# One core, a hybrid decoder layer: head 0 by quarter products, a stacked operand for the sample's pooling columns, small rows on another queue

## The chip, the cores and the metric

The kernel runs on one core of one Trainium2 chip. The metric is the device time of one execution in microseconds (us), the median of several runs. TensorE (PE) multiplies, VectorE (DVE), ScalarE (ACT) and GpSimd (POOL) do the elementwise work, and DMAs are issued from the queues of SyncE (SP) and of ScalarE. All numbers are float32. A product of two float32 matrices is made of three products of a faster format: each operand is split into a rounded part `hi` and the remainder `lo`, and `hi*hi + hi*lo + lo*hi` are summed in PSUM.

## The reference, cut to what matters

```python
u = x * (1 + scale1) + shift1            # scale1, shift1 from silu(c) @ w_ada + b_ada
z = u @ w_in                             # columns: pool | q | f | i | out_gate | gate_A | gate_B
# A: pooling over the "pool" columns;  B: per head a recurrence from q, f, i, then norm and out_gate
f = lb + (1.0 - lb) * sigmoid(z_f);  q = silu(z_q);  v = z_i
merged = sigmoid(z_ga) * (y_pool @ w_a) + sigmoid(z_gb) * (y_hgrn @ w_b)
x = layer_norm(ALPHA * x + g1 * (merged @ w_out))
x = layer_norm(ALPHA * x + g2 * (silu(h @ w_gate) * (h @ w_up)) @ w_down)   # h = x*(1+scale2)+shift2
```

There is one prompt of 512 tokens and a sample group of 8 times 8 = 64 tokens, 576 columns in all; the model width is 1024, with 8 heads of 128.

## The kernel before

The weights pass once from HBM through SBUF; activations stand transposed, channels on the partitions and the 576 tokens (`T`) along the row. `UH` and `UL` (L247, L248) are the two parts of `u`, in eight row blocks `kt`.

**The start (L94 to L430).** SP's queue carries, in this order of the program: the conditioning rows `cc`, the first half of x, the first block of `w_ada`, six small loads into the tile `rows` (biases, norm weights; L282 to L285), the next block of `w_ada`, the first slice of `w_in`, and then further blocks of `w_ada`, x and `w_in`. PE transposes x and `rows`, multiplies `c` by `w_ada` in pairs of blocks (`ada1`, L359), and the results `mod` give scale and shift. For b = 0 to 3 the loop at L389 makes two row blocks of `u` with their parts, calls `ada1` for the next b, and multiplies the two blocks by the 512 pooling columns of `w_in` into five accumulators `ps0` (tile `zp`, L417): four of 128 prompt tokens and one of the 64 sample tokens, three products of 512 columns each. VectorE also makes the sums `ta`, `tb`, `tc_` of blocks of `u` (L420 to L425), which `split` (L171) parts into `TU["t1"]`, `"t2"`, `"t4"` and later `"t3"`.

**Head 0 (L484 to L516 and L755 to L766).** The four column blocks f, q, i, out_gate of head 0 are made by `gemm` (L158): eight row blocks times three products times two column halves (256 and 320), 48 matmuls each. The weight of a `gemm` comes by `load_w` (L114): one load and one split (ACT a cast, DVE a difference). Between the four stand the pooling products `mix(0)` to `mix(3)` (L463), and then the elementwise work `ev_f`, `ev_q`, `ev_qd` of head 0's recurrence. The load of f is held until the last block of `w_ada` is issued (`late`, L493).

**Heads 1 to 7 (from L767).** Two column blocks at a time are made by `fast_u` (L744) and `fast` (L220): with weights and activations cut in quarters, seven products of 12 matmuls with 288 columns make both. The weights of such a pair, `fast_w` (L182) and `fast_q`, take two loads (the second into `rawu`, which has one buffer), four sums or differences of quarters (`s1` to `s4`; for these pairs on GpSimd), casts on ACT, and differences on DVE and GpSimd. They come into three buffers each of `whi` and `wlo`, in turn, and `hq`, `lq` with one. The pair after is prepared while one is multiplied. Inside the pairs stand the steps of the head before (`hg1` to `hg4`).

The order of instructions on each engine is fixed before the run: a planner simulates the program and places every instruction when it deems it ready, in the program's order of priority. On the chip each engine takes its instructions in that order and waits where an operand isn't there. The rest of the kernel (the gates, `w_b`, `w_out`, the feed-forward layer) is not touched.

Of the kernel before, what the change touches and what calls it, by code (L numbers as in the profile page):

```python
# [73 lines left out]
def trunk(tc, consts, x_prompt, x_sample, state_pool, state_hgrn, c_prompt, c_sample,  # L74
# [16 lines left out]
    U, _U = pl.open("u", "left")  # L91
    s0, _s0 = pl.open("s0", "right")
    sx, _sx = pl.open("sx", "right")
    cc = t_(s0, [9, D], "cc")  # L94
    sp.dma_start(out=cc[0:1], in_=c_prompt)
    sp.dma_start(out=cc[1:9], in_=c_sample)
    cst = t_(cp, [P, C_END], "cst")
    act.dma_start(out=cst, in_=consts[:, 0:C_END])
    ident = cst[:, C_ID:C_ID + P]
    rows = t_(s0, [92, P], "rows")  # L100
    R_LB, R_NW, R_PS, R_BA, R_LG, R_LO, R_END = 0, 16, 24, 28, 76, 84, 92
    cst_eps = t_(cp, [P, 2], "eps")
    dve.memset(cst_eps[:, 0:1], RMS_EPS)
    dve.memset(cst_eps[:, 1:2], LN_EPS)
# [174 lines left out]

    xin = [x_load(0)]  # L280
    ada_ready[SC1 // 2] = ada_load(s0, SC1 // 2)
    for r, src in ((R_BA, b_ada[0]), (R_LB, lb_logits.rearrange("r c -> (r c)")), (R_NW, hgrn_norm_w[0]),  # L282
                   (R_PS, pool_scale[0]), (R_LG, ln1_g[0]), (R_LO, ln1_b[0])):
        v = src.rearrange("(h p) -> h p", p=P)
        sp.dma_start(out=rows[r:r + v.shape[0]], in_=v)  # L285
    ada_ready[SH1 // 2] = ada_load(s0, SH1 // 2)
    w0 = [load_w(seq.pop(0))]
    ada_pre(1)
# [87 lines left out]
    dve.tensor_tensor(out=oml, in0=le1, in1=oml, op=ALU.mult)  # L376
    dve.tensor_scalar(out=noml, in0=oml, scalar1=-1.0, scalar2=None, op0=ALU.mult)

    YA = t_(ym, [P, 4, T], "ya")
    YB = t_(ym, [P, NH, T], "yb")  # L380


    ta = YB[:, 0:2].rearrange("p a (k n) -> p (a k) n", n=HT)
# [2 lines left out]
    def t_tiles(p, names):  # L386
        return {n: tuple(t_(p, [P, 4, HT], n + x, F32R) for x in "hl") for n in names}

    for b in range(4):  # L389
        us_ = []  # L390
        for kt in (2 * b, 2 * b + 1):

            sc, sh = mod[:, SC1 + kt], mod[:, SH1 + kt]
            u = YB[:, 2 + kt] if b < 2 else t_(s0, [P, T], "u32", bufs=2)
            us_.append(u)
            us = u[:, TP:T].rearrange("p (b l) -> p b l", b=NB)
            act.activation(out=UH[:, kt, 0:TP], in_=XT[:, kt, 0:TP], func=AF.Identity, scale=sc[:, 0:1], bias=sh[:, 0:1])
            dve.tensor_tensor(out=us, in0=XT[:, kt, TP:T].rearrange("p (b l) -> p b l", b=NB),
                              in1=bcast(sc[:, 1:9], LS), op=ALU.mult)
            dve.tensor_tensor(out=us, in0=us, in1=bcast(sh[:, 1:9], LS), op=ALU.add)  # L400
            dve.tensor_copy(out=UH[:, kt, TP:T], in_=u[:, TP:T])
            act.activation(out=u[:, 0:TP], in_=XT[:, kt, 0:TP], func=AF.Identity, scale=sc[:, 0:1], bias=sh[:, 0:1])
            dve.tensor_tensor(out=UL[:, kt], in0=u, in1=UH[:, kt].bitcast(F32), op=ALU.subtract)
        if b < 3:
            ada1(b + 1)
        if b == 0:
            x_turn(1)
            pl.close(_sx)
            tu, _tu = pl.open("tu", "left")
            TU = t_tiles(tu, ("t1", "t2", "t4"))  # L410
        for kt in (2 * b, 2 * b + 1):
            hi, lo = (half(x, kt % 2) for x in w0[b])
            for i in range(5):
                n = P if i < 4 else TS
                xh, xl = (x[:, kt, i * P:i * P + n] for x in (UH, UL))
                for j, (x, w) in enumerate(((xh, lo), (xl, hi), (xh, hi))):
                    pe.matmul(out=ps0[i][:n], lhsT=x, rhs=w, start=kt + j == 0, stop=kt == KT - 1 and j == 2)  # L417
        for u, kt in zip(us_, (2 * b, 2 * b + 1)):
            if b < 2:
                dve.tensor_tensor(out=ta[:, kt], in0=u[:, HT:T], in1=u[:, 0:HT], op=ALU.subtract)  # L420
            else:
# [41 lines left out]
    def mix(g):  # L463
        c = slice(g * P, (g + 1) * P)
        own, first, prev, buf, smp = (bnd[:, g, a:b] for a, b in
                                      ((D_W, D_1), (D_1, D_P), (D_P, D_B), (D_B, D_S), (D_S, D_END)))
        ps = st_()
        px = st_()
        pe.matmul(out=ps[:, 0:16], lhsT=ZT[:, 0, c], rhs=first, start=True, stop=True)
        pe.matmul(out=ps[:, 16:P], lhsT=ZT[:, 0, c], rhs=own[:, 16:], start=True, stop=True)  # L470
        for i in range(1, 4):
            pe.matmul(out=ps[:, i * P:(i + 1) * P], lhsT=ZT[:, i, c], rhs=own, start=True, stop=False)
            pe.matmul(out=ps[:, i * P:i * P + 16], lhsT=ZT[:, i - 1, c], rhs=prev, start=False, stop=True)
        pe.matmul(out=px[:, :TS], lhsT=spt[:, c], rhs=buf, start=True, stop=False)
# [9 lines left out]
    for i in range(5):  # L484
        n = P if i < 4 else TS
        (dve.tensor_copy if i % 2 else act.copy)(out=ZT[:n, i], in_=ps0[i][:n])
    for n, t, k0, k1 in (("t2", tb, 2, 4), ("t4", ta, 0, 4)):
        split(*(x[:, k0:k1] for x in TU[n]), t[:, k0:k1])
    pl.close(_psA)
    psB, _psB = pl.open("psB", "right", space=PSUM)  # L490
    psZ, _psZ = pl.open("psZ", "left", space=PSUM)
    z = zt()
    with tc.issue_after(late.ins):  # L493
        w = next_w()
    gemm(z, w, UH, UL)
    wu, _wu = pl.open("wu", "left")
    for n, k, c in (("b11", 0, 0), ("b21", 4, 0), ("b12", 0, HT), ("b22", 4, HT)):
        TU[n] = tuple(x[:, k:k + 4, c:c + HT] for x in (UH, UL))
    TU["t3"] = TU["b12"]
    f0 = YB[:, 6]  # L500
    act.activation(out=f0, in_=z[:, ZR], func=AF.Sigmoid)
    mix(0)
    mix(1)
    z = zt()
# [85 lines left out]
    def ev_i(h, v):  # L590
        H[h].update(v=v, vx=stack3(v, "vx", (0, 2), 1))
# [124 lines left out]
    def ada_late(m, pl_):  # L716
# [15 lines left out]
        for j in range(4):  # L732
# [7 lines left out]
    pairs = iter([(win(a + h), win(b + h)) for h in range(1, NH) for a, b in ((M_F, M_Q), (M_I, M_OG))] +  # L740
                 [(win(M_GA + m), win(M_GB + m)) for m in range(KT)])
    ready_f = []

    def fast_u(g, u, mid=None, end=None):  # L744

        q = ready_f.pop()
        for specs in pairs:
            ready_f.append(fast_w(specs, wu, 2, eng=pool, lo34=pool))
            break
        fast(q, TU, f_, g, u, mid, end)  # L750
# [568 lines left out]
```

## Time and profile before

| | us |
|---|---|
| median of 3 runs | 1029.49 (1029.02 to 1033.24) |
| the profiled execution | 1027.83 |
| its span in the trace | 1025.6 |
| PE busy over the span | 973.9 (95%) |
| DVE busy | 785.0 (77%) |
| ACT busy | 495.6 (48%) |
| POOL busy | 366.5 (36%) |

A busy share counts the time in which an engine has an instruction under way; for PE the ends are modelled, so the share of a stretch and the distance from one matmul's start to the next are read together. PEld is PE's loading of the stationary operand, which overlaps the matmuls.

### The profile page before, as it was taken

To read this page: it belongs to the slowest core of one execution; us is meant where nothing else is said; L and a number is where in the kernel's file an instruction comes from. 1 tells how busy PE (TensorE), PEld (TensorE's weight loads), DVE (VectorE), ACT (ScalarE), POOL (GpSimd) and SP (SyncE) were. 2 spreads that over 40 slices of the span, in tenths; PEclk is the share of its full clock that TensorE was granted. 3 is DMA by queue.
4 is the path that set the end of the run, shared out by engine and by line. 5 is a ranking of instruction groups with operands and counts; after the bars stand their busy time and mean duration, and the time that the engine had idled before them with its cause. 6 is when DMAs were issued, how large, how long until landed. Compare 5 with 4: busy or idle time off the path is not lost.

```text
span 1025.6 us, 17312 instructions
## 1 busy us (share of the span) xinstructions
PE 973.9 (95%) x6675; PEld 888.9 (87%) x6675; DVE 785.0 (77%) x1341; ACT 495.6 (48%) x897; POOL 366.5 (36%) x271
## 2 busy tenths in 40 slices
PE   6999999999999999998989998999999999999993
PEld 3789899999999997788987788999999999788882
DVE  3653989988898664359796879999999998947428
ACT  3454675567655663343333355444444446433322
POOL 0013776668675765633661102222222220000004
PEclk9999999999999999998999999999999999999997
DMA  8950233324332359942228302232332334322202
GB/s 282 300 151 23 80 109 106 86 86 123 87 105 86 106 185 308 303 150 82 83 83 257 103 1 62 65 101 83 104 103 83 98 100 142 121 89 81 78 14 92
DMA packets 158116, 120.54 MB, mean 118 GB/s; under 512 B 3933, under 2 KB 137081, under 8 KB 158027
## 3 DMA queue, kind: packets, MB, share of 16 engines
q1 hardware_dynamic: 155695, 113.98, 36.6%
q10 hardware_dynamic: 2340, 5.47, 1.6%
q8 instruction: 52, 0.85, 0.3%
q14 instruction: 29, 0.24, 0.1%
HBM read 111.15 MB, written 8.40 MB: 117 GB/s over the span
## 4 chain that ended last, share of the span: by engine, by line
PE 65%; DVE 18%; DMA 5%; issue 5%; ACT 4%; POOL 2%; SPq 0%; POOLq 0%; DVEq 0%; ACTq 0%
PE b L217 24%; PE f L217 12%; PE b L1164 4%; PE b L1163 4%; PE b L1162 4%; PE z L154 3%; PE zp L417 3%; DMA ada<-in_w_ada 2%; DVE tmp L560 2%; ACT whi L172 2%; DVE wlo L173 2%; PE s L723 1%; DVE S L658 1%; PE b L1168 1%; PE b L1167 1%
## 5 line engine op out<-in xcount | busy, mean ns | idle before, releaser
L172 ACT CAST whi<-st 128x512 fp32r<-128x512 f32 x184 | 108.8, 617 | 55.7 <-PE b L217 13.3
L173 DVE TENSOR_TENSOR wlo<-st,whi 128x512 fp32r<-128x512 f32 x140 | 113.8, 838 | 9.4 <-ACT whi L172 4.2
L217 PE MATMUL f<-uh,whi 128*128 128x288 f32 x352 | 105.8, 301 | 0.0
L217 PE MATMUL f<-ul,whi 128*128 128x288 f32 x352 | 104.9, 298 | 0.0
L197 POOL TENSOR_TENSOR st<-raw 128x512 f32<-128x512 f32 x36 | 53.5, 1487 | 142.2 <-DVE wlo L173 61.4
L217 PE MATMUL f<-uh,wlo 128*128 128x288 f32 x352 | 104.1, 296 | 0.0
L172 ACT CAST whi<-raw 128x1024 fp32r<-128x1024 f32 x46 | 48.3, 1050 | 98.8 <-PE b L217 55.5
L112 DVE TENSOR_TENSOR wlo<-raw,whi 128x1024 fp32r<-128x1024 f32 (+1 forms) x49 | 57.9, 1182 | 36.8 <-ACT whi L111 36.4
L111 ACT CAST whi<-raw 128x1024 fp32r<-128x1024 f32 (+1 forms) x49 | 48.0, 979 | 66.4 <-PE b L1164 20.0
L198 POOL TENSOR_TENSOR st<-st,raw 128x512 f32<-128x512 f32 x46 | 63.2, 1373 | 38.3 <-issue 35.7
L173 DVE TENSOR_TENSOR wlo<-raw,whi 128x1024 fp32r<-128x1024 f32 x46 | 58.6, 1274 | 19.0 <-ACT whi L172 18.9
L203 POOL TENSOR_TENSOR st<-raw,st 128x512 f32<-128x512 f32 x26 | 42.5, 1634 | 84.3 <-DVE wlo L173 84.3
L1164 PE MATMUL b<-whi,hl 128*128 128x512 f32 (+1 forms) x198 | 72.6, 367 | 0.0
L1163 PE MATMUL b<-whi,hl 128*128 128x512 f32 (+1 forms) x198 | 72.5, 366 | 0.0
L1162 PE MATMUL b<-wlo,hl 128*128 128x512 f32 (+1 forms) x198 | 72.4, 365 | 0.0
L217 PEld LDWEIGHTS f<-uh,whi 128*128 128x128 f32 x352 | 66.1, 188 | 4.6 <-issue 1.7
L217 PEld LDWEIGHTS f<-ul,whi 128*128 128x128 f32 x352 | 66.1, 188 | 3.5 <-issue 3.4
L217 PEld LDWEIGHTS f<-uh,wlo 128*128 128x128 f32 x352 | 66.1, 188 | 2.8 <-issue 2.5
L1231 POOL TENSOR_TENSOR x<-x,lg 128x640 f32<-128x640 f32 (+2 forms) x4 | 5.9, 1468 | 164.6 <-ACT x L1222 164.6
L173 POOL TENSOR_TENSOR wlo<-st,whi 128x512 fp32r<-128x512 f32 x44 | 58.4, 1337 | 5.4 <-ACT whi L172 4.6
L217 PE MATMUL b<-bh,whi 128*128 128x288 f32 x184 | 55.2, 300 | 2.1 <-ACT bh L172 2.1
L217 PE MATMUL b<-bl,whi 128*128 128x288 f32 x184 | 54.6, 297 | 0.0
(461 smaller groups left out, 3251.8 us busy)
## 6 DMA issues: line engine op xcount, KB each, us to landing
raw<-in_w_in SPq DMA_DIRECT2D x52, 512.0 KB
ada<-in_w_ada SPq DMA_DIRECT2D x16, 1024.0 KB
raw<-in_w_gate SPq DMA_DIRECT2D x22, 512.0 KB
raw<-in_w_down SPq DMA_DIRECT2D x22, 512.0 KB
ada<-in_w_ada SPq DMA_DIRECT2D x16, 512.0 KB
raw<-in_w_up SPq DMA_DIRECT2D x12, 512.0 KB
rawu<-in_w_up SPq DMA_DIRECT2D x10, 512.0 KB
s<-in_state_hgrn SPq DMA_DIRECT2D x8, 512.0 KB
```

Source lines behind the costliest of these rows:

```text
L111: act.copy(out=hi[:, :n], in_=raw[:, :n])
L112: eng.tensor_tensor(out=lo[:, :n], in0=raw[:, :n], in1=hi[:, :n].bitcast(F32), op=ALU.subtract)
L154: mm = pe.matmul(out=ps[:, GA0 + c0:GA0 + c1], lhsT=a[:, kt * P:(kt + 1) * P], rhs=x[:, kt, c0:c1], start=first and i == 0, stop=last and ...
L172: act.copy(out=hi, in_=src)
L173: return eng.tensor_tensor(out=lo, in0=src, in1=hi.bitcast(F32), op=ALU.subtract)
L197: pool.tensor_tensor(out=s1, in0=a21, in1=a22, op=ALU.add)
L198: pool.tensor_tensor(out=s2, in0=s1, in1=a11, op=ALU.subtract)
L203: eng.tensor_tensor(out=s4, in0=a12, in1=s2, op=ALU.subtract)
L217: pe.matmul(out=ps, lhsT=x[:, k * P:(k + 1) * P], rhs=y[:, k], start=first and k + i == 0, stop=last and k == 3 and i == 2)
L1162: pe.matmul(out=o, lhsT=xh, rhs=lo, start=first, stop=False)
L1163: pe.matmul(out=o, lhsT=xl, rhs=hi, start=False, stop=False)
L1164: return pe.matmul(out=o, lhsT=xh, rhs=hi, start=False, stop=last)
```

## The change

Three edits, with the order of the text moved accordingly:

1. Head 0's f and q, and its i and out_gate, are made as two pairs by `fast_u`, as for the other heads. The pool `wu` of the weights opens earlier, the bank pool `psF` takes the place of `psZ`, `t3` is split before head 0, and no load is held for `late` any more. `mix(0)` and `mix(1)` stand inside the first pair, `mix(2)` and `mix(3)` behind it.
2. For the 64 sample tokens, both parts of `u` stand side by side in a tile `UX` (64 columns hi, 64 columns lo). One matmul multiplies all 128 by the weight's `hi`, one multiplies the 64 hi columns by `lo`: two in place of three per row block. The two halves of the result are added after.
3. The two loads of `cc` and the six of `rows` are issued from ACT's queue, at the very start; `cc` lies in a part of `YB` that is free then.

```diff
-    sp.dma_start(out=cc[0:1], in_=c_prompt)
-    sp.dma_start(out=cc[1:9], in_=c_sample)
+    act.dma_start(out=cc[0:1], in_=c_prompt)
+    act.dma_start(out=cc[1:9], in_=c_sample)
...
+        act.dma_start(out=rows[r:r + v.shape[0]], in_=v)
...
-        sp.dma_start(out=rows[r:r + v.shape[0]], in_=v)
...
+            dve.tensor_copy(out=UX[:, kt, 0:TS], in_=u[:, TP:T])
+            dve.tensor_tensor(out=UX[:, kt, TS:P], in0=u[:, TP:T], in1=UX[:, kt, 0:TS].bitcast(F32), op=ALU.subtract)
...
-            for i in range(5):
+            for i in range(4):
...
+            o, w, x = ps0[4], (hi, lo), UX[:, kt]
+            for j in (0, 1) if kt < KT - 1 else (1, 0):
+                if j:
+                    pe.matmul(out=o[:TS], lhsT=x[:, :TS], rhs=lo, start=False, stop=False)
+                else:
+                    pe.matmul(out=o, lhsT=x, rhs=hi, start=kt == 0, stop=kt == KT - 1)
...
+    ready_f.append(fast_w(next(pairs), wu, 2, eng=pool, lo34=pool))
...
+    act.copy(out=ZT[:TS, 4], in_=ps0[4][TS:])
+    dve.tensor_tensor(out=ZT[:TS, 4], in0=ps0[4][:TS], in1=ZT[:TS, 4], op=ALU.add)
...
-    with tc.issue_after(late.ins):
-        w = next_w()
-    gemm(z, w, UH, UL)
...
-    gemm(z, next_w(), UH, UL)
+    psF, _psF = pl.open("psF", "left", space=PSUM)
+    f0, q0 = YB[:, 6], YB[:, 7]
+    fast_u(f0, q0, lambda: (mix(0), mix(1)), lambda: act.activation(out=f0, in_=f0, func=AF.Sigmoid))
+    act.activation(out=q0, in_=q0, func=AF.Silu)
...
-    gemm(z, next_w(), UH, UL)
-    act.copy(out=v, in_=z[:, ZR])
-    ev_i(0, v)
...
-    gemm(z, w, UH, UL)
-    act.copy(out=g, in_=z[:, ZR])
+    fast_u(v, g, None, lambda: (ev_qd(0), ev_i(0, v)))
```

## Rows read from the trace of the kernel before

**Rows 1.** The page: busy time, share of the span and instructions of each engine.
```profile
PE 973.9 (95%) x6675; PEld 888.9 (87%) x6675; DVE 785.0 (77%) x1341; ACT 495.6 (48%) x897; POOL 366.5 (36%) x271
```

**Rows 2.** Busy times by stretch: from:to and length, then each engine's.
```profile
23.71:63.47 39.76, 39.57 (x248) 28.88 (x245) 28.31 (x66) 20.12 (x28) 1.05 (x2) 1.00 0.80 246
63.47:101.84 38.37, 38.37 (x290) 37.51 (x288) 12.05 (x20) 18.66 (x30) 11.08 (x13) 1.00 0.31 81
101.84:134.20 32.36, 29.30 (x232) 27.99 (x231) 29.89 (x47) 18.04 (x35) 21.44 (x18) 1.00 0.32 87
...
167.00:199.90 32.90, 32.22 (x256) 31.24 (x256) 29.19 (x52) 21.82 (x46) 22.34 (x18) 1.00 0.35 99
```

**Rows 3.** PE's instructions in order of time: start, duration, engine, line, out<-in.
```profile
56.60 1.32 PE L417 MATMUL zp<-wlo,uh 128*64 128x512 f32 x5
...
59.58 0.40 PE L417 MATMUL zp<-whi,ul 128*64 128x512 f32 x1
...
60.04 1.31 PE L417 MATMUL zp<-wlo,uh 128*128 128x512 f32 x5
...
63.47 0.42 PE L154 MATMUL z<-uh,whi 128*128 128x256 f32 x2
...
69.86 0.29 PE L469 MATMUL s<-bnd,zt 128*128 128x16 f32 x2
...
101.84 0.29 PE L217 MATMUL f<-uh,whi 128*128 128x288 f32 x1
...
106.59 0.29 PE L217 MATMUL f<-t1h,whi 128*128 128x288 f32 x1
```

**Rows 4.** SP's queue in order of time: start and duration of the issues.
```profile
0.74 0.35 SPq L95 DMA_DIRECT2D cc<-in_c_prompt  x1
...
4.34 2.12 SPq L257 DMA_DIRECT2D ada<-in_w_ada  x2
6.50 0.50 SPq L285 DMA_DIRECT2D rows<-in_b_ada  x1
...
10.94 1.83 SPq L257 DMA_DIRECT2D ada<-in_w_ada  x2
```

**Rows 5.** Busy times in steps of 2 us; the last two are DMA share and GB/s.
```profile
10.00:12.00 2.00, 1.83 (x14) 1.31 (x12) 0.69 (x1) 0.91 (x3) 0.00 (x0) 1.00 0.54 161
12.00:14.00 2.00, 0.75 (x9) 0.52 (x12) 0.23 (x1) 0.87 (x1) 0.00 (x0) 1.00 0.87 265
...
18.00:20.00 2.00, 2.00 (x15) 1.43 (x7) 0.76 (x4) 0.33 (x1) 0.00 (x0) 1.00 1.08 358
```

**Rows 6.** PE in order of time ahead of the first pooling product; in brackets its waits.
```profile
13.60 0.39 PE L352 MATMUL t<-cst,rows 92*128 92x92 f32 x1 [1.25 <-DMA rows<-in_ln_b]
...
17.56 1.08 PE L339 MATMUL t<-ada,cpad 128*32 128x256 f32 x8 [0.86 <-DMA ada<-in_w_ada]
...
23.72 2.41 PE L417 MATMUL zp<-wlo,uh 128*128 128x512 f32 x5
```

**Rows 7.** VectorE's small operations by line, shapes apart: count, busy, mean ns.
```profile
L398 DVE TENSOR_TENSOR u<-xt,mod 128x64 f32<-128x64 f32 x4 | 0.8, 219 | 0.0
...
L401 DVE CAST uh<-u 128x64 fp32r<-128x64 f32 x4 | 0.6, 192 | 0.0
```

**Rows 8.** The waits of PE in 101.8 to 137: total, times, longest.
```profile
PE s L609 <- POOL kl L564: 1.4, 1, 1.4
```

**Rows 9.** The chain that ended last, by time: a pair's load and GpSimd's sums.
```profile
103.72 3.86 DMA raw<-in_w_in
107.72 1.51 POOL st L197
...
112.23 1.26 POOL st L198
```

**Rows 10.** VectorE by time: one operation beside GpSimd's and between them.
```profile
107.99 1.85 DVE L562 TENSOR_TENSOR kd<-tmp,tmp 128x576 f32<-128x576 f32 x1
...
159.75 0.75 DVE L562 TENSOR_TENSOR kd<-tmp,tmp 128x576 f32<-128x576 f32 x1
```

More of the change, by code (lines that the diff above doesn't have):

```diff
@@ L93, in trunk @@
     sx, _sx = pl.open("sx", "right")
-    cc = t_(s0, [9, D], "cc")
-    sp.dma_start(out=cc[0:1], in_=c_prompt)
-    sp.dma_start(out=cc[1:9], in_=c_sample)
+    YA = t_(ym, [P, 4, T], "ya")
+    YB = t_(ym, [P, NH, T], "yb")
+    cc = YB[0:9, 6:8].rearrange("p a n -> p (a n)")[:, 0:D]
+    act.dma_start(out=cc[0:1], in_=c_prompt)
+    act.dma_start(out=cc[1:9], in_=c_sample)
     cst = t_(cp, [P, C_END], "cst")
@@ L101, in trunk @@
     R_LB, R_NW, R_PS, R_BA, R_LG, R_LO, R_END = 0, 16, 24, 28, 76, 84, 92
+    for r, src in ((R_BA, b_ada[0]), (R_LB, lb_logits.rearrange("r c -> (r c)")), (R_NW, hgrn_norm_w[0]),
+                   (R_PS, pool_scale[0]), (R_LG, ln1_g[0]), (R_LO, ln1_b[0])):
+        v = src.rearrange("(h p) -> h p", p=P)
+        act.dma_start(out=rows[r:r + v.shape[0]], in_=v)
     cst_eps = t_(cp, [P, 2], "eps")
@@ L132, in trunk @@
     win = lambda m: ("c", w_in[0], m, KT)
-    seq = [("h", w_in[0], (0, k), 2) for k in range(KT // 2)] + [win(M_F), win(M_Q), win(M_I), win(M_OG)]
+    seq = [("h", w_in[0], (0, k), 2) for k in range(KT // 2)]
     gate_up = lambda m: (("c", w_gate[0], m, KT), ("c", w_up[0], m, KT))
@@ L281, in trunk @@
     ada_ready[SC1 // 2] = ada_load(s0, SC1 // 2)
-    for r, src in ((R_BA, b_ada[0]), (R_LB, lb_logits.rearrange("r c -> (r c)")), (R_NW, hgrn_norm_w[0]),
-                   (R_PS, pool_scale[0]), (R_LG, ln1_g[0]), (R_LO, ln1_b[0])):
-        v = src.rearrange("(h p) -> h p", p=P)
-        sp.dma_start(out=rows[r:r + v.shape[0]], in_=v)
     ada_ready[SH1 // 2] = ada_load(s0, SH1 // 2)
@@ L377, in trunk @@
     dve.tensor_scalar(out=noml, in0=oml, scalar1=-1.0, scalar2=None, op0=ALU.mult)
-    YA = t_(ym, [P, 4, T], "ya")
-    YB = t_(ym, [P, NH, T], "yb")
+    UX = t_(s0, [P, KT, P], "ux", F32R)
     ta = YB[:, 0:2].rearrange("p a (k n) -> p (a k) n", n=HT)
@@ L410, in trunk @@
             TU = t_tiles(tu, ("t1", "t2", "t4"))
+            wu, _wu = pl.open("wu", "left")
         for kt in (2 * b, 2 * b + 1):
             hi, lo = (half(x, kt % 2) for x in w0[b])
-            for i in range(5):
-                n = P if i < 4 else TS
-                xh, xl = (x[:, kt, i * P:i * P + n] for x in (UH, UL))
+            for i in range(4):
+                xh, xl = (x[:, kt, i * P:(i + 1) * P] for x in (UH, UL))
                 for j, (x, w) in enumerate(((xh, lo), (xl, hi), (xh, hi))):
-                    pe.matmul(out=ps0[i][:n], lhsT=x, rhs=w, start=kt + j == 0, stop=kt == KT - 1 and j == 2)
+                    pe.matmul(out=ps0[i], lhsT=x, rhs=w, start=kt + j == 0, stop=kt == KT - 1 and j == 2)
+            o, w, x = ps0[4], (hi, lo), UX[:, kt]
[4 more added lines that the diff above has]
+                    pe.matmul(out=o, lhsT=x, rhs=hi, start=kt == 0, stop=kt == KT - 1)
         for u, kt in zip(us_, (2 * b, 2 * b + 1)):
@@ L430, in trunk, with fast_u @@
     pl.close(_s0)
+    pairs = iter([(win(a + h), win(b + h)) for h in range(NH) for a, b in ((M_F, M_Q), (M_I, M_OG))] +
+                 [(win(M_GA + m), win(M_GB + m)) for m in range(KT)])
+    ready_f = []
+    def fast_u(g, u, mid=None, end=None):
+        q = ready_f.pop()
+        for specs in pairs:
+            ready_f.append(fast_w(specs, wu, 2, eng=pool, lo34=pool))
+            break
+        fast(q, TU, f_, g, u, mid, end)
     def zt():
@@ L482, in mix @@
             act.activation(out=YA[:, g, c0:c1], in_=ps[:, :c1 - c0], func=AF.Copy, scale=prow[:, R_PS + g:R_PS + g + 1])
[L484 to L487, printed above, removed]
+    ready_f.append(fast_w(next(pairs), wu, 2, eng=pool, lo34=pool))
+    for i in range(4):
+        (dve.tensor_copy if i % 2 else act.copy)(out=ZT[:, i], in_=ps0[i])
+    act.copy(out=ZT[:TS, 4], in_=ps0[4][TS:])
+    dve.tensor_tensor(out=ZT[:TS, 4], in0=ps0[4][:TS], in1=ZT[:TS, 4], op=ALU.add)
+    for n, k, c in (("b11", 0, 0), ("b21", 4, 0), ("b12", 0, HT), ("b22", 4, HT)):
+        TU[n] = tuple(x[:, k:k + 4, c:c + HT] for x in (UH, UL))
+    TU["t3"] = TU["b12"]
+    for n, t, k0, k1 in (("t2", tb, 2, 4), ("t4", ta, 0, 4), ("t3", tc_, 0, 4)):
         split(*(x[:, k0:k1] for x in TU[n]), t[:, k0:k1])
@@ L490, in trunk @@
     psB, _psB = pl.open("psB", "right", space=PSUM)
-    psZ, _psZ = pl.open("psZ", "left", space=PSUM)
-    z = zt()
-    with tc.issue_after(late.ins):
-        w = next_w()
-    gemm(z, w, UH, UL)
[L496 to L504, printed above, removed]
-    gemm(z, next_w(), UH, UL)
-    q0 = YB[:, 7]
-    q0_ = act.activation(out=q0, in_=z[:, ZR], func=AF.Silu)
+    psF, _psF = pl.open("psF", "left", space=PSUM)
+    f0, q0 = YB[:, 6], YB[:, 7]
+    fast_u(f0, q0, lambda: (mix(0), mix(1)), lambda: act.activation(out=f0, in_=f0, func=AF.Sigmoid))
+    act.activation(out=q0, in_=q0, func=AF.Silu)
     mix(2)
@@ L738, in trunk @@
     ada_todo = [SC2, SC2 + 4, SH2, SH2 + 4, G1, G1 + 4, G2, G2 + 4]
[L740 to L750, printed above, removed]
-    v, g = vg()
-    zt()
-    z = zt()
-    gemm(z, next_w(), UH, UL)
-    act.copy(out=v, in_=z[:, ZR])
-    ev_i(0, v)
-    z = zt()
-    w = next_w()
-    ready_f.append(fast_w(next(pairs), wu, 2, eng=pool, lo34=pool, hold=q0_))
-    gemm(z, w, UH, UL)
-    act.copy(out=g, in_=z[:, ZR])
+    v, g = vg()
+    fast_u(v, g, None, lambda: (ev_qd(0), ev_i(0, v)))
     ev_og(0, g)
-    split(*TU["t3"], tc_)
-    pl.close(_psZ)
-    psF, _psF = pl.open("psF", "left", space=PSUM)
     for h in range(1, NH):
```

## The prediction

> **What bounds the kernel now.** I read the page first, then busy times by stage, and then, inside the stages that the change touches, PE's order of time, SP's queue and the DMA share. The page says that PE is busy nearly throughout [rows 1]. A share over a whole kernel hides stages with other limits, so the stretches matter [rows 2]: from the first pooling product (23.71) to head 0's first `gemm` (63.47) PE is busy 39.57 of 39.76 us; in head 0's four `gemm`s with the four `mix` (63.47 to 101.84) it never rests; in head 1 (to 134.20) it rests 32.36 - 29.30 = 3.06 us; in a later head (167.00 to 199.90) only 0.68. So work taken from PE ahead of 101.84 should shorten the kernel, as long as no load or preparation becomes the later one. Ahead of 23.71 the loads lead: PE waits for `rows` at 13.60 and for a block of `w_ada` at 17.56 [rows 6].
>
> **The change part by part.**
>
> **Head 0.** A `gemm` is 48 matmuls; the first runs from 63.47 to 69.86, 6.39 us, 0.133 each [rows 3]. Four are 25.56 us. A pair is 7 times 12 = 84 matmuls; 36 of them (three products) lie between 101.84 and 106.59, so one is 4.75 / 36 = 0.132 and the two pairs 168 * 0.132 = 22.17 us. That is 24 matmuls fewer, and **3.4 us** off PE, where PE is without a rest [rows 2]. Against that, a pair needs what a `gemm` doesn't: every pair in a later head comes with waits, 0.68 us for a head's two [rows 2]. I charge head 0 the same, **-0.7**. The four `mix` keep their work. The preparation is new at this place: eight GpSimd sums, six GpSimd differences and the casts of two pairs, in a stretch where GpSimd had 11.08 of 38.37 and VectorE 12.05. For the first pair the first two sums can run as soon as both loads are there, during the pooling products, where GpSimd does 1.05 of 39.76. If that cover is gone, it costs what rival 3 says. `t3`'s split comes earlier, into VectorE's last part of the pooling stretch (28.31 of 39.76 busy); it is needed by the sixth product, five products of 1.58 us after the pair's start, which hide it; without them it is paid in full, a larger split than any in my rows.
>
> **The sample's pooling products.** In one row block 15 matmuls take 60.04 - 56.60 = 3.44 us, 0.229 each. The last two, with only 64 stationary columns, start at 59.58 and end the block at 60.04: 0.23 each as well [rows 3]. So 128 stationary columns cost what 64 do, and one in three of the sample's products, 8 in all, goes: 8 * 0.229 = **1.8 us**, in a stretch where PE is busy all but 0.19 us. Added are eight casts and eight differences of 64 columns on VectorE, 8 * (0.192 + 0.219) = 3.3 us [rows 7], which bring VectorE from 28.31 to 31.6 of 39.76 there, so I cost them at nothing; PE's backlog covers them, and if the backlog went, 3.3 is the price. The two evacuations of the sample's sum replace one and hide behind the pair's first products. The Trainium skill (Perfetto Trace Analysis, Identifying the Most-Contended Engine) holds matmul busy time to be a poor measure of PE's limit and asks for the weight loads' share instead. By that rule PE has room in this stretch (28.88 of 39.76, 73%) and none in the next (37.51 of 38.37), and the term would be 0.73 * 1.8 = 1.3 and the whole gain 6.8 rather than 7.3. I keep 1.8, because the distance from start to start shows matmuls back to back.
>
> **The small rows.** In SP's queue the two `cc` loads stand ahead of x, and the six `rows` loads between two blocks of `w_ada`: the block is issued at 10.94 and not at 6.50 [rows 4]. In that gap the DMA share falls to 0.54 and 0.87, against 1.08 once the queue is full [rows 5]. Moved to ACT's queue, they free 10.94 - 6.50 = 4.4 us of SP and the 0.74 us that x waits for `cc` (it can then be issued where `cc` was). How much earlier does PE's 23.71 come? Not below nothing: no transfer is added, and SP's order is otherwise kept. At most 4.4 + 0.7 = 5.1, if the block's issue alone decides. The transfers themselves move up by what the DMA engines idled: (1.08 - 0.54) / 1.08 * 2 + (1.08 - 0.87) / 1.08 * 2 = 1.4, and 0.7 of head start: **2.1 us**. I take this, since the later blocks of `w_ada`, x and `w_in` follow in the same stream, and PE's 39.76 us behind it can't outrun it for long. On ACT the eight issues stand ahead of the conditioning's sigmoid. They take no more than the 4.4 us they took on SP; the cover is PE's own wait until 13.60 for these very rows, and 4.4 is the price without it. The wait for `rows` at 13.60 (1.25) falls away with the move; it is not added, since PE waits again at 17.56 for the block.
>
> **What comes after.** The step `hg1` of head 0 waited 1.4 us for GpSimd's `kl` [rows 8], and head 1 rests 2.4 us more than a later head [rows 2]. With the change `mix(3)`, whose space the recurrence's tiles take, is finished earlier, but PE arrives earlier too. Bounds: 2.4 gained, 1.4 lost once more; I take **0.7** gained, a little above the middle, since head 0 becomes like a later head.
>
> **Sum:** 3.4 - 0.7 + 1.8 + 2.1 + 0.7 = 7.3 us. On the profiled execution: a span of 1018.3 from 1025.6, a time of 1020.5 from 1027.83. The median lies 1.7 above that execution, so 1029.5 - 7.3 = **1022.2**.
>
> **The rivals.**
>
> 1. **The start doesn't move PE.** For it: between 23.71 and 63.47 PE follows an order fixed by the planner, and VectorE's 3.3 us of new work lie in the same steps that make `u`. Then the 2.1 are lost: 1024.3. Chance 0.20.
> 2. **VectorE and GpSimd in each other's way.** One and the same difference took 0.75 us and, with GpSimd at work, 1.85 [rows 10]. GpSimd gets 14 operations more in head 0; at 1.1 us each that is 15 us, against 26 us that VectorE has free there, so most hides; three on the chain cost 3.3: 1025.5. The Trainium skill (SBUF — State Buffer, Who interferes with whom) says that a VectorE instruction with two SBUF inputs contends with GpSimd's reads and that the later one fully blocks; the two durations agree. Chance 0.12.
> 3. **Slower: the preparation stands exposed.** `rawu` has one buffer: the next pair's load waits until GpSimd has done with the last, and then take 3.86 (load), 1.51 and 1.26 (sums) [rows 9], 6.6 us ahead of the second product; less the first product's 1.58, 5.0 us a pair. It decides from the point where GpSimd is done with a pair later than 5.0 us ahead of the next one's start. Against it: later heads run like this with 0.68 us of rest. If head 0's two pairs both pay, 10.1 - 7.3 = 2.8 slower: 1032.3; with head 1's first pair, 1037.3. Chance 0.08.
> 4. **The start gives more**, the block's issue deciding: 5.1 in place of 2.1, 1019.2. Chance 0.12.
>
> **How the numbers follow.** The forecast has 0.48. A measurement tells 0.5% (5.1 us) from no change, so faster means under 1024.3. Of the forecast 0.42 lies there, of rival 1 half, 0.10, of rival 2 0.03, of rival 4 all: 0.67. Slower means over 1034.6: half of rival 3, 0.04. The rest is 0.29. The range runs from 1016.5 (rival 4 with the 2.4 of head 1 in place of 0.7, and a little) to 1028.0 (rival 2 without the start's 2.1, and a little); rival 3 lies outside, and some 0.06 of the others.
>
> **What would show it.** Right: the DMA share holds near 1.08 from 8 us on, the first pooling product starts near 21.6; 112 pooling matmuls end near 59.5; two pairs and four `mix` take some 35.5 us. Wrong: PE waiting for `whi` or `t2` in head 0's pairs (rivals 2, 3), a first pooling product at 23 or one at 19 (rivals 1, 4), or head 1 resting over 3 us.

## The result, and the profile after

The changed kernel takes 1034.76 us (median of 10 runs, 1033.54 to 1040.52), the kernel before 1028.54 beside it. The medians are 6.2 us apart; the means, from which all ratios here are made, 7.8 us: a ratio of 1.0075, 95% interval 1.0057 to 1.0092. It is slower, where 7.3 us less were forecast. (One of the ten executions of the kernel before took 3329.88 us and is left out of the ratio.) The profiled execution is the slowest of the ten, 1040.52 us with a span of 1038.7; a second profile of the same kernel (after_again, below) has a span of 1036.0 and the same stretches ahead of 150 us to within 0.2 us.

First the busy line of the page, and the busy times by stretch, as in [rows 1] and [rows 2]: pooling, head 0, head 1, and a later head.

```profile
PE 971.7 (94%) x6643; PEld 887.9 (85%) x6643; DVE 802.9 (77%) x1377; ACT 499.4 (48%) x905; POOL 386.4 (37%) x285
```

```profile
25.85:64.12 38.27, 35.89 (x224) 27.03 (x221) 30.82 (x77) 20.51 (x28) 7.12 (x4) 1.00 0.67 196
64.12:108.68 44.56, 37.73 (x265) 36.44 (x264) 16.47 (x32) 21.20 (x37) 24.64 (x26) 0.92 0.36 98
108.68:149.57 40.89, 35.11 (x252) 33.83 (x250) 38.61 (x58) 20.33 (x44) 27.28 (x20) 0.92 0.28 79
182.22:215.12 32.90, 32.23 (x256) 31.25 (x255) 29.16 (x52) 21.81 (x47) 23.22 (x18) 1.00 0.35 99
```

In [rows 2] head 1 is cut off at 134.20, inside its second pair. Head 2 starts at 136.79, so head 1 before is longer than the prediction took it to be, with the same 3.06 us of rest:

```profile
101.84:136.79 34.95, 31.89 (x251) 30.58 (x250) 32.48 (x50) 19.80 (x45) 24.03 (x20) 1.00 0.34 93
```

PE has less to do, as forecast, and rests more. Against before: the first pooling product comes 2.1 us later (25.85 and 23.72), the pooling stretch is 1.5 shorter (38.27 and 39.76), head 0 is 6.2 longer (44.56 and 38.37), and head 1 5.9 longer (40.89 and 34.95). A later head takes the same 32.90. So the loss lies ahead of 150 us: head 3 starts 12.2 us later than before, and the end comes 13.1 us later (10.4 in after_again). The medians and means stand less far apart than the traces; what the unprofiled executions do better can't be seen.

VectorE's column is the one to remember: 16.47 of 44.56 in head 0, 38.61 of 40.89 in head 1. PE's waits from 0 to 150 us (what waited, for what; total, times, longest), cut to those that matter:

```profile
PE t L306 <- DMA cst<-in_consts: 8.7, 1, 8.7
PE f L223 <- DVE zt L510: 6.0, 1, 6.0
PE f L223 <- DVE g L236: 2.4, 1, 2.4
PE s L694 <- DVE S L672: 2.0, 1, 2.0
...
PE s L681 <- DVE atp L656: 1.3, 1, 1.3
```

And the granted clock (third number from the end of the line) behind three of these rests:

```profile
72.00:76.00 4.00, 4.00 (x17) 4.00 (x18) 0.04 (x1) 0.40 (x1) 2.55 (x2) 0.50 0.83 181
117.00:121.00 4.00, 3.36 (x14) 3.36 (x15) 4.00 (x9) 1.58 (x4) 2.30 (x3) 0.57 0.37 112
141.00:145.00 4.00, 4.00 (x24) 4.00 (x22) 4.00 (x7) 0.36 (x2) 1.41 (x1) 0.57 0.56 159
```

PE works at the lower of its two levels (0.50, 1.2 GHz) for some 4.8, 3.4 and 3.4 us, and loses half of each. Head 0: 38.37 - 3.4 (fewer matmuls) + 6.0 (wait) + 2.4 (clock) + 0.9 (a wait for `v`) = 44.3 of the 44.56. Head 1: 34.95 + 3.4 (clock) + 2.7 (PE's rests, 40.89 - 35.11 = 5.8 for 3.06) = 41.1 for the 40.89.

**Head 0's wait**, in order of time on four engines (start, duration, engine, line, out<-in, in brackets the wait):

```profile
60.90 1.28 DVE L179 TENSOR_TENSOR wlo<-st,whi 128x512 fp32r<-128x512 f32 x2
...
63.14 1.34 DVE L179 TENSOR_TENSOR ul<-yb,uh 128x1152 fp32r<-128x1152 f32 x1
64.41 1.35 DVE L179 TENSOR_TENSOR t4l<-yb,t4h 128x1152 fp32r<-128x1152 f32 x1
```
```profile
61.72 5.16 POOL L209 TENSOR_TENSOR st<-raw,st 128x512 f32<-128x512 f32 x1 [8.44 <-DVE wlo L179]
66.96 1.26 POOL L211 TENSOR_TENSOR st<-raw,raw 128x512 f32<-128x512 f32 x1
```
```profile
68.26 1.14 ACT L178 CAST whi<-st 128x512 fp32r<-128x512 f32 x2 [4.51 <-POOL st L211]
69.30 1.06 ACT L508 COPY zt<-zp 128x512 f32<-128x512 f32 x2
70.38 0.58 ACT L509 COPY zt<-zp 64x512 f32<-64x512 f32 x1
```
```profile
71.82 0.58 PE L223 MATMUL f<-t2h,whi 128*128 128x288 f32 x1 [5.96 <-DVE zt L510]
```

Read it from the bottom. The pair's second product needs a PSUM bank that still holds a pooling sum. That sum is evacuated on ACT at 69.30 to 70.96 and added on VectorE. ACT's order has two casts of the pair's preparation ahead of the evacuations, and these wait 4.51 us for GpSimd's difference, which is late because the one before it took 5.16 us. The same operation in second_pair (below), where VectorE was adding from PSUM, with one input in SBUF:

```profile
116.40 1.29 POOL L209 TENSOR_TENSOR st<-raw,st 128x512 f32<-128x512 f32 x1
```

While it was under way for 5.16 us, VectorE did sums and differences with two SBUF inputs without a pause, the last of them until 65.76; GpSimd was done 1.1 us later. The Trainium skill (SBUF — State Buffer, Who interferes with whom) says that such an instruction contends with GpSimd's reads; the trace agrees, with 5.16 against 1.29 us.

**The start.** PE's first transposes, and ACT's queue:

```profile
1.64 0.39 ACTq L100 DMA_DIRECT2D cst<-in_consts  x1
...
8.61 0.26 ACTq L107 DMA_DIRECT2D rows<-in_pool_scale  x1
...
13.10 1.05 ACT L318 ACTIVATE sc<-yb 9x1024 f32<-9x1024 f32 x1
```
```profile
8.72 1.94 PE L306 MATMUL t<-cst,x 128*128 128x128 f32 x8 [8.72 <-DMA cst<-in_consts]
```

The constants, which hold the identity for the transposes, are now third in ACT's queue and land at 8.7 us; before, the first transposes began at 5.03. The issues of the six loads of `rows` hold ACT until 10.6, so the sigmoid of the conditioning comes at 13.10, and not at 4.15, as in the kernel before:

```profile
4.15 1.05 ACT L316 ACTIVATE sc<-cc 9x1024 f32<-9x1024 f32 x1 [1.49 <-DMA cc<-in_c_sample]
```

The first pooling product is no clean mark of how far PE is. With edit 3, two groups of 32 `w_ada` matmuls stand ahead of it, and before it was 48 in all; the other 16 then ran inside the pooling stretch, which is one reason why that stretch is now shorter:

```profile
17.28 3.64 PE L341 MATMUL t<-ada,cpad 128*32 128x256 f32 x32
...
22.66 3.26 PE L341 MATMUL t<-ada,cpad 128*32 128x256 f32 x32
```

### The profile page after: what moved, and what is told of

It is laid out like the page before. It is cut to its first block, busy times and chain, and to the rows that moved or that the text cites. A ratio compares the mean times of both kernels' runs of the same rounds, so it can differ in the third digit from the quotient of the medians.

```text
span 1038.7 us, 17325 instructions
## 1 busy us (share of the span) xinstructions
PE 971.7 (94%) x6643; PEld 887.9 (85%) x6643; DVE 802.9 (77%) x1377; ACT 499.4 (48%) x905; POOL 386.4 (37%) x285
## 4 chain that ended last, share of the span: by engine, by line
PE 67%; DVE 20%; issue 4%; DMA 4%; ACT 4%; POOL 1%; ACTq 0%; DVEq 0%; POOLq 0%
PE b L223 24%; PE f L223 16%; PE b L1154 4%; PE b L1153 4%; PE b L1152 4%; DVE wlo L179 2%; DMA ada<-in_w_ada 2%; PE z L160 2%; DVE tmp L574 2%; DVE S L672 1%; PE s L737 1%; ACT whi L178 1%; DVE qz L601 1%; PE zp L420 1%; PE b L1158 1%
## 5 line engine op out<-in xcount | busy, mean ns | idle before, releaser
L178 ACT CAST whi<-st 128x512 fp32r<-128x512 f32 x192 | 113.5, 617 | 62.4 <-PE f L223 14.8
L223 PE MATMUL f<-uh,whi 128*128 128x288 f32 x384 | 116.9, 304 | 3.3 <-DVE g L236 2.4
L223 PE MATMUL f<-ul,whi 128*128 128x288 f32 x384 | 115.3, 300 | 0.0
L223 PE MATMUL f<-uh,wlo 128*128 128x288 f32 x384 | 114.3, 298 | 0.0
L209 POOL TENSOR_TENSOR st<-raw,st 128x512 f32<-128x512 f32 x28 | 48.0, 1716 | 109.6 <-DVE wlo L179 107.1
L223 PEld LDWEIGHTS f<-uh,whi 128*128 128x128 f32 x384 | 73.2, 191 | 8.7 <-DVE g L236 4.1
L118 DVE TENSOR_TENSOR wlo<-raw,whi 128x1024 fp32r<-128x1024 f32 (+1 forms) x45 | 53.0, 1177 | 33.1 <-ACT whi L117 32.8
L223 PEld LDWEIGHTS f<-ul,whi 128*128 128x128 f32 x384 | 73.3, 191 | 3.5 <-issue 3.4
L223 PEld LDWEIGHTS f<-uh,wlo 128*128 128x128 f32 x384 | 73.1, 190 | 2.8 <-issue 2.5
L179 POOL TENSOR_TENSOR wlo<-st,whi 128x512 fp32r<-128x512 f32 x48 | 65.5, 1372 | 9.6 <-ACT whi L178 8.8
```

The costliest lines, as they stand in the source:

```text
L118: eng.tensor_tensor(out=lo[:, :n], in0=raw[:, :n], in1=hi[:, :n].bitcast(F32), op=ALU.subtract)
L209: eng.tensor_tensor(out=s4, in0=a12, in1=s2, op=ALU.subtract)
L223: pe.matmul(out=ps, lhsT=x[:, k * P:(k + 1) * P], rhs=y[:, k], start=first and k + i == 0, stop=last and k == 3 and i == 2)
```

## The experiments

"Alone" means put into the kernel before without the other edits. The ratios are to the kernel before, measured beside each.

**One edit at a time.** rows_alone has edit 3, sample_alone edit 2, head_alone edit 1.

> The kernel before with the third edit alone (the two cc loads and the six rows loads issued from ScalarE's queue). Theory A (the move hurts the start: the constants' load stands behind the cc loads and beside x, ScalarE waits in its queue for the small loads, and the first pooling product comes 2.1 us later, as in the changed kernel, 25.85 against 23.71): 1028.5 + 2.1 = 1030.6, and a constants landing well behind 3.7 us. Theory B (the late start is an accident of the one profiled execution): the first product at 23.7 or earlier, 1026.4 to 1028.5.

> The kernel before with the second edit alone (both parts of the sample's u side by side, 112 pooling matmuls for 120; cc lies in yb, still loaded by SyncE). Theory A (PE's term was right): 1028.5 - 1.8 = 1026.7, the stretch from the first pooling product to head 0's first product 1.5 to 1.8 us shorter than 39.76. Theory C (the 3.3 us of small VectorE operations lie on the chain that makes u): no gain or a loss up to 3.3, 1028.5 to 1031.8, and PE waiting for ul.

> The kernel before with the first edit alone (head 0 by two pairs), as the change has it, with ev_qd(0) twice. Theory A (the stall of 6 us in the first pair comes from an order of ScalarE in which the casts of s3 and s4 stand ahead of the evacuations of the pooling sums; here two evacuations stand ahead of the first cast): no wait over 2 us in the first pair, head 0 in 36 to 38 us for 38.37, but head 1 still some 5.9 longer for the work done twice: 1028.5 - 1.5 + 5.9 = 1033. Theory D (the preparation of the pairs itself is exposed, as rival 3 of the prediction): a wait of 5 us or more in the first pair whatever the order, 1036 to 1039.

Measured: rows_alone 0.9964 (0.9950 to 0.9977), sample_alone 0.9980 (0.9959 to 1.0000), head_alone 1.0077 (1.0056 to 1.0098). The small edits gain 3.7 us (2.4 to 5.1) and 2.0 (0 to 4.2), and the whole loss is in head 0's edit. Theory A of rows_alone falls; A of sample_alone has the time. In the traces both small edits start head 0 1.8 us earlier (61.68 and 61.66, 63.47 before), but the first pooling product hardly moves (23.32 and 23.07, 23.72 before). What rows_alone gains beyond 1.8 us can't be placed. head_alone has a pooling stretch of 42.2 us (39.76 before), head 0 of 39.0 and head 1 of 40.9; theory A has head 1 and the missing wait but not the time (1036.51), D the time but not the wait. Here ACT's order had two of the evacuations ahead of those casts and PE's wait there was 0.7 us, and the clock kept full in head 0. So head 1's loss doesn't hang on that wait.

**The doubled step.** The changed kernel calls `ev_qd(0)` twice, at L613 and at the end of the second pair. once drops the first call:

```diff
     ev_f(0, f0)
     ev_q(0, q0)
-    ev_qd(0)
```

> The changed kernel without the first of its two calls of ev_qd(0), so that the three products of q with the decay are made once, in the second pair. Theory A (the work done twice, 2.84 + 0.21 and 1.61 + 0.32 us of VectorE ahead of kd, makes PE wait 2.4 us in head 1's first pair, which drops to the low clock after it): head 1's first pair to head 2's first pair 35 us for 40.9, 1034.8 - 5.9 = 1029. Theory E (head 1 is long because head 0's recurrence starts late, after mix(3), whatever is done twice): at most the 3 us of VectorE, 1032 to 1034.8.

Measured: 1.0066 (1.0043 to 1.0090), 1035.28 us. The doubled work costs nothing that can be told from the times, and theory A falls. In the trace head 1 is 2.1 us shorter, 38.78, and its clock stays full, but the pooling stretch is 1.3 longer. All experiments on the changed kernel below start from once.

**Both small edits without head 0's (rows_sample).**

> The kernel before with the two small edits (the sample's pooling products side by side, the small rows on ACT's queue) and with head 0's four gemm as before. Alone they gave -2.0 and -3.7 us. If they add up, from a median of 1028: 1022.3. If both only move the same start of PE: 1024.3. If the lost time of the changed kernel comes from the two small edits together, and not from head 0: above 1028.

Measured: 0.9968 (0.9948 to 0.9987), 1025.06 us. They don't add up:

```profile
24.54:61.63 37.09, 35.32 (x224) 27.20 (x221) 28.10 (x76) 19.71 (x26) 0.53 (x1) 1.00 0.79 237
61.63:100.00 38.37, 38.37 (x289) 37.51 (x288) 13.32 (x22) 18.90 (x31) 11.48 (x14) 1.00 0.33 93
100.00:134.79 34.79, 31.92 (x252) 30.61 (x251) 32.31 (x50) 19.81 (x45) 24.06 (x20) 1.00 0.33 94
```

Head 0 starts at 61.63, as with either edit alone. PE, which rested 0.19 us in the pooling stretch before and 1.25 in rows_alone, rests 1.77 now: it waits for `ul` (0.9) and for the evacuated products of `w_ada` (0.8). Against rows_alone the 1.8 us of the second edit are gone from PE's work, but the first pooling product comes 1.2 us later (24.54 and 23.32) and PE rests 0.5 more.

**Constants first.** rs_cst_first moves the constants' load to the head of ACT's queue.

```diff
+    act.dma_start(out=cst, in_=consts[:, 0:C_END])
     act.dma_start(out=cc[0:1], in_=c_prompt)
     act.dma_start(out=cc[1:9], in_=c_sample)
-    act.dma_start(out=cst, in_=consts[:, 0:C_END])
```

> Both small edits with the constants' load put ahead of the small rows on ACT's queue. In both small edits' kernel PE's first transposes wait for the constants until 8.7 us (5.0 before). Theory L (the pooling stretch ends when u is there, and u follows the stream of loads): the transposes come 3 us earlier, the last pooling product stays within 0.5 us of 61.2, and the time is 1024 to 1026. Rival M (PE's late start is what keeps the two gains from adding): the stretch ends 2 us earlier, 1022 to 1023.

Measured: 0.9974 (0.9951 to 0.9996), 1025.51 us. The transposes come at 4.54, the first pooling product at 24.44 as in rows_sample, and head 0 at 60.61, 1.0 us earlier. The time is no shorter. Theory L has the time, but the stretch did end 1 us earlier, and here the granted clock was 0.54 to 0.61 from 22 to 26 us, where rows_sample has 1.00; what sets the stretch's end is not settled.

**Halves of head 0's edit.** Both have the small edits. second_pair makes f and q by `gemm` and i and out_gate by a pair; first_pair the reverse (it also leaves out `ev_qd(0)`, so its output lacks head 0's products with q).

> Both small edits, and of head 0's edit a half: F and Q by gemm as before, I and output gate by a pair. Theory F (VectorE sets the length of the stretch from the recurrence's first operation to head 2, and the second pair's eight adds and its preparation lie in that stretch): head 1's two pairs stay some 40 us long as in the whole change (35 before), 1022.3 - 1.7 + 5 to 6 = 1026 to 1027. Theory H (the loss is made by the first pair: ACT's order behind GpSimd's differences, and a recurrence that starts late): head 1 falls back to 35, and the time is 1022.3 - 1.7 = 1020.6.

> Both small edits, and the other half: F and Q by a pair, I and output gate by gemm. Theory F: head 1 falls back to some 35 us, and only head 0's stall of 6 us at the pair's second product stays: 1022.3 - 1.7 + 6 = 1026 to 1027. Theory H: nearly the whole loss stays, 1033 to 1035.

Measured: second_pair 0.9999 (0.9981 to 1.0017), first_pair 1.0083 (1.0058 to 1.0108), where rows_sample has 0.9968. first_pair's three stretches, to be held against those of rows_sample above:

```profile
24.53:64.28 39.75, 36.26 (x224) 26.97 (x221) 31.04 (x77) 21.29 (x29) 7.23 (x4) 1.00 0.68 201
64.28:108.59 44.31, 38.36 (x277) 37.30 (x276) 16.90 (x30) 19.42 (x33) 18.20 (x20) 0.92 0.35 99
108.59:146.22 37.63, 33.38 (x252) 32.36 (x251) 31.86 (x48) 19.71 (x46) 24.33 (x19) 0.95 0.33 93
```

The first pair costs at three places: 2.7 us in pooling, 5.9 in head 0 with the 6.0 us wait, 2.8 in head 1, where the clock falls after a rest. The second pair alone costs 4.0 in head 1 (38.80) and gains 0.5 in head 0 (37.87). Neither F nor H holds as written: F has the second pair's head 1 right, H that the first pair's half makes most of the loss.

**What holds PE in head 1.** VectorE in once, where head 1 starts at 109.35, and the wait that it makes:

```profile
108.10 2.36 DVE L571 TENSOR_TENSOR_SCAN p<-yb,d 128x576 f32<-128x576 f32 x1
110.38 0.79 DVE L236 TENSOR_TENSOR g<-f,g 128x288 f32<-128x288 f32 x2
111.10 3.76 DVE L574 RECIPROCAL tmp<-p 128x192 f32<-128x192 f32 x3
114.78 2.84 DVE L601 TENSOR_TENSOR qz<-yb,p 128x256 f32<-128x256 f32 x2
117.54 0.21 DVE L602 TENSOR_TENSOR qs<-yb,p 128x64 f32<-128x64 f32 x1
117.67 0.21 DVE L588 TENSOR_TENSOR vx<-v,vx 128x64 fp32r<-128x64 f32 x1
117.81 0.44 DVE L236 TENSOR_TENSOR g<-f,g 128x288 f32<-128x288 f32 x1
```
```profile
118.31 0.40 PE L223 MATMUL f<-uh,whi 128*128 128x288 f32 x1 [2.44 <-DVE g L236]
```

The last of the second pair's seven adds (L236 at 117.81; the expectation above counts eight) empties the bank for which PE waits, ahead of the fifth product of head 1's first pair. It stands behind 6.7 us of the recurrence and of `vx`. A `gemm` is emptied by one copy on ACT and has no such adds.

**Evacuations ahead of the preparation (evac_first).**

```diff
-    ready_f.append(fast_w(next(pairs), wu, 2, eng=pool, lo34=pool))
     for i in range(4):
         (dve.tensor_copy if i % 2 else act.copy)(out=ZT[:, i], in_=ps0[i])
...
     TU["t3"] = TU["b12"]
+    ready_f.append(fast_w(next(pairs), wu, 2, eng=pool, lo34=pool))
```

> The changed kernel without the doubled ev_qd(0), and with the evacuations of the pooling sums ahead of the last two casts of the first pair's preparation in ACT's order. Theory J (the first pair's second product waits 5 to 6 us because ACT stands in front of those casts until GpSimd has made the differences, and the clock falls after that rest): that wait goes under 1.5 us and the low clock behind it too, head 0 falls from 42.9 to some 38 us, and the time from 1035.3 to 1030 to 1031, the rest of the loss staying in the pooling stretch and in head 1. Rival (the wait only moves to the casts' own products, four and six, which need them): head 0 stays above 41.5 us and the time at 1034 or more.

Measured: 1.0031 (1.0011 to 1.0051), 1032.77 us. PE's waits in head 0:

```profile
66.32 0.37 PE L223 MATMUL f<-t2h,whi 128*128 128x288 f32 x1 [1.85 <-DVE zt L509]
...
72.97 0.41 PE L496 MATMUL s<-bnd,spt 128*128 128x64 f32 x2 [1.54 <-DMA spt<-in_state_pool]
```

And on GpSimd and ACT ahead of them, to be held against the rows of head 0's wait:

```profile
60.35 5.16 POOL L209 TENSOR_TENSOR st<-raw,st 128x512 f32<-128x512 f32 x1 [8.44 <-DVE wlo L179]
```
```profile
62.93 1.08 ACT L507 COPY zt<-zp 128x512 f32<-128x512 f32 x2 [0.56 <-PE zp L427]
```

5.1 us (in once) have become 1.85, the clock stays full, and head 0 is 40.84 instead of 42.92. GpSimd's difference takes 5.16 us as ever, but the evacuations no longer stand behind it; what is left of the wait is VectorE's own order, with its splits ahead of the add at 65.50. Theory J is right in kind and somewhat too large: a new wait of 1.54 us for `spt` takes part of it. Head 1 stays at 38.80.

**All four mix early (early_mix).** `mix(2)` and `mix(3)` are put beside `mix(0)` and `mix(1)`, inside the first pair.

> The changed kernel without its doubled step ev_qd(0), and with all four mix between the first pair's third and fourth product, so that the memory that the recurrence of head 0 takes is free earlier. If head 1's length is set by when the recurrence starts (theory G), its two pairs shrink by what the recurrence's first operation comes earlier ahead of them, up to the 5.9 us: 1035 - 5 = 1030. If it is set by what VectorE has to do behind that start while PE's products wait for its adds (theory F), head 1 stays within 1.5 us of 40.9: 1034 to 1035.

Measured: 1.0084 (1.0053 to 1.0115). This told nothing on G: the mixes kept their pace of some 6 us each, the last output began at 102.23 (102.81 in once), and the recurrence's first operation followed 1.3 us behind it as ever. Head 1 stayed at 38.8.

**VectorE relieved in head 1.** In second_pair_norecip and rows_sample_norecip the three reciprocals of head 0 are left out, and `kd` is made from their input:

```diff
         for c0, c1 in ((0, 192), (192, 384), (384, T)):
-            dve.reciprocal(out=r[:, c0:c1], in_=pp[:, c0:c1])
+            if h:
+                dve.reciprocal(out=r[:, c0:c1], in_=pp[:, c0:c1])
```

> Both small edits and the second pair alone, without the three reciprocals of head 0's recurrence (3.9 us of VectorE; they are left out, so head 0's numbers are others). Theory F (VectorE is the bound from the recurrence's start to head 2): head 1 shortens from 38.8 us by some 3 to 4, and the time from 1028.4 to 1024.5 to 1025.5. Rival K (head 1 is long because GpSimd's preparation or the loads come late): within 1 us of 38.8, and 1028.

> The control for it: both small edits, head 0 by gemm, and the reciprocals of head 0 left out. If VectorE has room in head 1 as long as head 0 goes by gemm, head 1 stays at 34.8 us, less than 1 us shorter; if VectorE bounds head 1 there as well, it shortens by 2 us or more, toward the 32.9 of a later head.

Measured: second_pair_norecip 1.0000 (0.9979 to 1.0021), no gain; rows_sample_norecip has one execution, and only its trace is read. Head 1 did shorten with the pair, from 38.80 to 36.04, as F says, and in the control by 1.3 (33.5, between the two expectations). But with the pair head 2 gave it back, 35.5 us instead of 32.7. The order on ACT had come out otherwise, with a cast of `vx`, which needs VectorE's `v`, ahead of head 0's squares:

```profile
138.73 0.39 ACT L601 CAST vx<-v 128x64 fp32r<-128x64 f32 x2 [5.07 <-DVE v L236]
```

So this run can't decide F: removing the operations also changed the order.

**The recurrence earlier (early_f).** Based on evac_first. Head 0's `k`, scan input and result, reciprocals and `kd` lie in slots of `YB` that are free by then, and not in the memory that `mix(3)` releases. No operation is taken away; one memset is added.

```diff
-        k = t_(ep, [P, T], "tmp", bufs=4)
+        k = t_(ep, [P, T], "tmp", bufs=4) if h else YB[:, 4]
...
-        pp = t_(hp, [P, T], "p", bufs=2)
+        pp = t_(hp, [P, T], "p", bufs=2) if h else YB[:, 2]
```

> The changed kernel without the doubled ev_qd(0), with the early evacuations, and with the products of head 0's recurrence (k, the scan's input and result, the reciprocals, kd) in free slots of YB and not in the memory that the last mix releases. So the recurrence can begin behind the first pair, when VectorE is mostly idle, and not 5 us ahead of head 1. Theory G (head 1 is long because VectorE meets the recurrence and the second pair's adds in one crowd): the adds' wait of 2.4 us ahead of head 1's second product goes, head 1 falls from 38.8 to 35 us or less, and the time from 1032.8 to 1028 to 1029. Rival K (head 1 is long because of its own two pairs and GpSimd's preparation): head 1 stays above 38 us, 1032 or more.

Measured: 0.9977 (0.9964 to 0.9991), 1026.53 us. Head 0 and head 1:

```profile
63.65:104.62 40.97, 36.51 (x265) 34.23 (x264) 25.39 (x38) 19.58 (x33) 29.42 (x29) 1.00 0.38 107
104.62:136.92 32.30, 31.24 (x251) 30.70 (x250) 27.64 (x49) 20.08 (x48) 23.21 (x18) 1.00 0.35 100
```

```profile
84.19 0.58 DVE L568 TENSOR_SCALAR yb<-yb,lbt 128x576 f32<-128x576 f32 x1 [0.16 <-ACT yb L567]
...
92.54 0.76 DVE L579 TENSOR_TENSOR yb<-yb 128x576 f32<-128x576 f32 x1
```

The recurrence, up to `kd`, runs from 84.19 to 93.3 instead of 98.36 to 113.5 in evac_first. Head 1 falls from 38.80 to 32.30, shorter than before the change, the wait for `g` is gone, and the time falls by 0.54% against evac_first, somewhat more than theory G said. G holds, and K falls: VectorE had the time, in head 0, where nothing was there for it to do. (The expectation calls the waiting product the second; it is the fifth, as in once.) Whether the same move would also shorten the kernel before, with its four `gemm`, was not run.

**The changed kernel again (after_again).**

> The changed kernel itself, for a profile of another execution. If the late start of its first profile (first pooling product at 25.9 us, constants landed at 8.7) is made by the queue's order, it shows again, within 0.5 us; if it is an accident of that execution, the first pooling product comes at 24.5 or earlier. The wait of 5 to 6 us at the first pair's second product and head 1 of 39 to 41 us should show in both cases.

Measured: 1.0075 (1.0046 to 1.0104). The first pooling product is at 25.88, the constants at 8.3, head 0 at 64.28 and head 1 at 108.96, and the waits of 6.0 and 2.4 us are there again: the late start belongs to the kernel.

None of the versions with a pair in head 0 beats rows_alone (0.9964) or rows_sample (0.9968). These two, rs_cst_first and early_f are all faster than both the kernel before and the changed one; their intervals overlap, so the four can't be ranked.

## Why the prediction was wrong

Two steps failed: one term put at nothing, the evacuations for which head 0's first pair waits, and one put at a gain, head 1.

**Head 0's 3.4 us** was somewhat large as PE's work and wrong as time. The 24 matmuls are gone, and PE's busy time fell by 3.0 us in the changed kernel, with the clock's 2.4 taken off its 37.73, but by only 1.9 to 2.2 where the clock stayed full (36.13 in head_alone to 36.51 in early_f, 38.37 before); why not by 3.4 is not shown. The step that failed is "The two evacuations of the sample's sum replace one and hide behind the pair's first products". I asked what covers these evacuations on PE's side and not what stands ahead of them in ACT's order: 6.0 us of wait and 2.4 of low clock. evac_first shows the order as the cause. The 0.7 us charged for the pairs' waits was taken from later heads, whose weights are prepared behind a full pair, not while VectorE makes `u` and its sums; even in early_f PE rests 4.5 us in head 0 (40.97 - 36.51), 1.8 of it still for that evacuation.

**The sample's products, 1.8 us:** borne out, as far as can be told. sample_alone gave 0.20%, some 2.0 us with an interval from 0 to 4.2, and head 0 starts 1.8 us earlier in its trace; 1.2 of that lies in the pooling stretch (38.59), which has the clock at 0.50 in its first 3 us. "I cost them at nothing" was right only for one edit at a time: in the changed kernel, with `t3`'s split and the pair's on top, VectorE has no free time left at the end of the pooling:

```profile
50.00:61.00 11.00, 9.45 (x41) 6.95 (x41) 11.00 (x29) 5.98 (x10) 3.20 (x3) 1.00 0.00 0
```

**The small rows, 2.1 us:** a gain of 3.7 alone, with half of the mechanism right. The loads did move up: SP issues the second half of x at 17.41 before, at 14.93 in rows_alone and at 16.03 with all edits, and head 0 starts 1.8 us earlier alone. But the first pooling product didn't come at 21.6: it came at 23.32 alone, and with all edits 2.1 us later than before. The cover that I named, PE's wait for `rows` at 13.60, was the wrong one. Two of the eight loads now stand ahead of the constants, and all eight ahead of the conditioning's sigmoid, both of which PE needs before 13.60. I priced the delay at 4.4 us at most; the sigmoid moved by 9.0. The pooling stretch became shorter instead (38.4 us alone), with 16 `w_ada` matmuls moved ahead of it.

**What comes after, 0.7 us gained:** the second step that failed, and a loss of 5.9 us in head 1 in its place. I compared head 0 with a later head ("becomes like a later head") without asking when its recurrence may begin. The warning stood in [rows 2]: VectorE 12.05 of 38.37 in head 0 and 29.89 of 32.36 in head 1. In rival 2 the 26 free microseconds were cover; but the recurrence waits for `mix(3)`'s memory, so the free time lies ahead of the work, and the seven adds of the second pair met a full queue. early_f shows it by moving that work into the free time.

**The rivals.** Rival 2 named the right engines but put 3.3 us on the chain and ended at 1025.5; the GpSimd operation on the chain took 3.9 us more than it does elsewhere, and only ACT's order put it on PE's path: in evac_first it is as slow, and PE waits 1.85 us. Rival 3, the one on the slower side, rested on a misreading, which stands ahead of the prediction too: the pairs of the heads load their second weight into `raw` with three buffers; `rawu` belongs to calls that ask for it. Its result (1032.3 to 1037.3) holds the measured time by chance only. I had not seen the doubled `ev_qd(0)`; with it head 1 is 2.1 us longer in the traces, and the times show no difference.

## What to carry to other kernels

Free time of an engine covers added work only if the work may start in it: ask which release (here memory, shared with the step before) lets it begin, and compare the stretch ahead of that point with the one behind. Where a change brings a product's preparation ahead of the emptying of a bank, look at the order on the engine that does both. To the price of a wait of PE, the slower clock that may follow is to be added.

## What the runs showed of the hardware

The granted clock fell to 0.50 during a rest of PE of 6.0 us (in after, at 69.8 us), and also behind a rest of 2.4 us (at 117.5 in after, 113 in evac_first) and one of 2.0 us (141.5 in after). Behind the same 2.4 us rest it stayed at 1.00 in once and in second_pair. So the price of one and the same wait was 2.4 us in some traces and some 4.1 in others.

A scan on VectorE took 2.36 us in once and 2.17 in early_f, where a GpSimd difference was under way as it began, and 1.36 in first_pair, where GpSimd was idle. Where the scan began first, it kept its 1.38 us and GpSimd's sum took 2.34 in place of some 1.28, as in after:

```profile
166.45 1.38 DVE L571 TENSOR_TENSOR_SCAN p<-tmp,d 128x576 f32<-128x576 f32 x1
```
```profile
166.57 2.34 POOL L203 TENSOR_TENSOR st<-raw 128x512 f32<-128x512 f32 x1
```
